# Sample's output projection as a job inside group 2, token sums added head by head, most final scalings on ACT

## The chip, the cores and the metric

One NeuronCore of one Trainium2 chip runs the program. The metric is the device time of one execution in microseconds. Engines are named as in the profile: PE multiplies matrices (PEld loads its weights), DVE, ACT and POOL are the vector, scalar and general engines, SP and POOL issue most of the DMAs. A name with a q (SPq, POOLq) is an engine's queue of issues.

## The reference

One layer over 1024 prompt tokens and 128 sample tokens (8 streams of 16), all in f32. The input is normalised and projected to q, k, v and gate of 8 stick-breaking heads (`sb`) and 8 retention heads (`ret`). Each branch's output is normalised per head, multiplied by the gain and SiLU of the gate, and both go through one output projection, are normalised and added to x:

```
def merge(o_sb, o_r, gate_sb, gate_r, g_sb, g_r, w_out):
    y_sb = head_rms_norm(o_sb, g_sb, gate_sb.dtype) * jax.nn.silu(gate_sb)
    y_r = head_rms_norm(o_r, g_r, gate_r.dtype) * jax.nn.silu(gate_r)
    y = jnp.concatenate([y_sb, y_r], axis=-1)
    return jnp.einsum('bte,ed->btd', y, w_out)
...
        xp = xp + rms_norm(out, norm_post[l])
```

## The kernel before

Tokens are worked in two groups: group 0 has prompt tiles 0 to 3 and the sample tile, group 1 (here called group 2, the second) has prompt tiles 4 to 7. For each group the heads follow one another; a written list (`order`, lines 203 to 214) gives the steps. rq, rk, rv, rg are the retention head's projections, q, k, v, sg the stick-breaking head's, x both value projections for two heads, ret starts a retention job.

Every product is made of three f32r products: each operand is split into a high part (ACT, line 137) and a low part (DVE, line 138). Weights come in blocks of 256 KB, `wr`, with four buffers, and their parts `wh` and `wl` with four each. A block of w_in feeds twelve matmuls of 512 columns.

Whatever is not a projection is a *job* (lines 164 to 184): a generator that does a piece and says after how many product steps it wants to go on. `tick()` counts a step after each product and lets one job go on, so that the jobs' instructions come to lie between the products. `drain` ticks until a job is done, with no products between. All engines work in order.

Head h of group 2: `stick_breaking` (line 657) computes scores (z), weights (sigmoids, a scan and a product into `be`), writes `be` to DRAM and reads it back in 32x32 blocks (`s_be`, lines 568 to 584), turns them on DVE into `kp` (line 587) and multiplies with the values (line 705). `finish` (line 631) normalises the head's output, takes it through DRAM in the same way, multiplies with the gate (line 649) and stores it to `s_y` (line 652).

Sample's output projection is four steps of the list, o4 to o7 (`do_o`, line 1166): 16 blocks of w_out each, and per block three matmuls into `acco` (line 1179). o4 follows head 4, o5 head 5, o6 and o7 stand in head 7 behind ret7. Their results go to `s_raw`; Sample's normalisation and addition of x (`finish_sample`, line 1392) comes in the final product.

The prompt's output projection is a block product in Winograd's form: tokens (group 0, group 2), heads (sb, ret) and output columns are halved, and seven products of sums replace eight. Sums of weights are made by the job `column_sums` (line 1216) and stored in `s_t`. Sums of token blocks, S1, S2, s3 and s4, are made by DMA alone in `row_sums` (line 1236): copies and adding copies of 1 MB, DRAM to DRAM, on POOL's queue. row_sums(0), heads 0 to 3, is a job from q6 of group 2; row_sums(1) is one in the final product. There are four units (two halves of the heads, two of the columns) of seven products of 48 matmuls, in the order "1265734", in the last unit "1265374"; each operand is loaded (`fill`, line 1246) and split (`cut`, line 1253) one or two products ahead. Product "1" of the first unit still belongs to the stretch of head 7.

At the end every output tile t (8) and column block c (4) is scaled by its row's factor and x is added, in one DVE instruction (line 1362), and stored: tiles 0 to 3 from `finish_first` (line 1384) behind product "3", tiles 4 to 7 one after the other during the last product "4".

## Time and profile before

| | |
|---|---|
| median of 3 runs | 2402.28 us (2400.89 to 2404.65) |
| the profiled execution | 2402.57 us, span 2400.9 us |
| PE busy | 2294.6 us, 13920 matmuls |
| DVE, ACT, POOL busy | 1423.1, 914.1, 544.0 us |
| DMA moved | 477.25 MB, 199 GB/s on average |

Times in the trace count from the span's start. A group line gives line, engine, operation, out<-in, count, busy time, mean ns, and the idle time of the engine just before with what ended it. A timeline line gives start, duration, engine, line, operation and, in brackets, the idle time before it and what released it. A line of waits gives the total, how often, and the longest.

### The profile page before, as it was taken

The page shows a single profiled execution, that of the slowest core. Times are in us where ns is not written, and L with a number is a line of the kernel's source. Part 1 is how long each engine was busy: PE and PEld are TensorE (multiplying, and loading weights), DVE is VectorE, ACT ScalarE, POOL GpSimd, SP SyncE. Part 2 cuts the span into 40 slices and gives each one's busy share as a digit, 9 for nine tenths or more (in the row PEclk, how much of TensorE's full clock was granted, in tenths as well). Part 3 has the DMA queues.
Part 4 walks back from the last instruction along what each step waited for, and adds up shares of the span by engine and source line. Part 5 has one row for each costly group of instructions (what it writes and reads, how often), then busy time and mean ns, then how long its engine had stood idle before and what let it go on. Part 6 is the DMA issues. An engine that isn't in the chain of part 4 may idle for free.

```text
span 2400.9 us, 38629 instructions
## 1 busy us (share of the span) xinstructions
PE 2294.6 (96%) x13920; PEld 2021.6 (84%) x13920; DVE 1423.1 (59%) x2772; ACT 914.1 (38%) x1889; POOL 544.0 (23%) x809
## 2 busy tenths in 40 slices
PE   7999999999999999999999999999999998969995
PEld 7999999999999999998888877887878876758884
DVE  8245565556455555558477767656565566535567
ACT  6333332324233332325343333434343345425342
POOL 2123231414142232414121121212122121110001
PEclk9999999999999999999999999999999999989998
DMA  7659687887779697889788988566578757775456
GB/s 244 162 140 235 159 191 169 188 194 175 182 161 231 149 202 165 192 208 238 206 238 264 271 262 251 145 155 175 157 201 229 190 169 234 246 215 184 135 203 236
DMA packets 698160, 477.25 MB, mean 199 GB/s; under 512 B 234640, under 2 KB 633232, under 8 KB 692272
## 3 DMA queue, kind: packets, MB, share of 16 engines
q1 hardware_dynamic: 623200, 316.27, 50.6%
q0 software_dynamic: 39568, 138.06, 21.2%
q10 hardware_dynamic: 35200, 20.45, 2.9%
q8 instruction: 109, 1.79, 0.3%
q14 instruction: 83, 0.68, 0.1%
HBM read 377.14 MB, written 114.29 MB: 205 GB/s over the span
## 4 chain that ended last, share of the span: by engine, by line
PE 77%; issue 7%; DMA 7%; DVE 5%; ACT 1%; POOL 1%; SPq 0%; DVEq 0%; ACTq 0%; POOLq 0%
PE acc L314 46%; PE accn L373 11%; PE a L1270 8%; PE accx L401 3%; PE pa L705 2%; PE z L672 2%; DMA wr<-w_out 1%; PE pd L841 1%; PE zc L776 1%; DMA s_s<-s_y 1%; DVE o L1362 1%; DVE kp L615 1%; DMA be<-s_bd 1%; DVE kp L587 1%; DMA out<-rawc 1%
## 5 line engine op out<-in xcount | busy, mean ns | idle before, releaser
L314 PE MATMUL acc<-mh,wh 128*128 128x256 f32 (+2 forms) x2304 | 662.0, 340 | 4.6 <-DVE rv L1156 4.1
L314 PE MATMUL acc<-mh,wl 128*128 128x256 f32 (+2 forms) x2304 | 663.1, 340 | 0.0
L314 PE MATMUL acc<-ml,wh 128*128 128x256 f32 (+2 forms) x2304 | 660.9, 339 | 0.9 <-DVE p0u L150 0.9
L138 DVE TENSOR_TENSOR wl<-wr,wh 128x512 fp32r<-128x512 f32 x432 | 296.2, 690 | 430.8 <-ACT wh L137 426.3
L137 ACT ACTIVATE wh<-wr 128x512 fp32r<-128x512 f32 x432 | 271.5, 632 | 631.5 <-PE acc L314 368.0
L314 PEld LDWEIGHTS acc<-mh,wh 128*128 128x128 f32 x2304 | 422.1, 188 | 40.3 <-issue 6.6
L314 PEld LDWEIGHTS acc<-mh,wl 128*128 128x128 f32 x2304 | 421.6, 188 | 36.9 <-issue 8.2
L314 PEld LDWEIGHTS acc<-ml,wh 128*128 128x128 f32 x2304 | 421.7, 188 | 36.3 <-issue 6.6
L757 POOL DMA_DIRECT2D kc<-cache_sb_k x256 | 166.5, 655 | 283.2 <-DVE kcT L788 131.2
L373 PE MATMUL accn<-whn,mh 128*128 128x256 f32 x768 | 223.9, 292 | 0.0
L373 PE MATMUL accn<-wln,mh 128*128 128x256 f32 x768 | 217.1, 283 | 0.0
L373 PE MATMUL accn<-whn,ml 128*128 128x256 f32 x768 | 217.0, 283 | 0.0
L373 PEld LDWEIGHTS accn<-whn,mh 128*128 128x128 f32 x768 | 146.7, 191 | 9.8 <-issue 7.9
L373 PEld LDWEIGHTS accn<-wln,mh 128*128 128x128 f32 x768 | 146.7, 191 | 0.3
L373 PEld LDWEIGHTS accn<-whn,ml 128*128 128x128 f32 x768 | 146.5, 191 | 0.0
L1270 PE MATMUL a<-wh,mh 128*128 128x512 f32 x320 | 126.2, 394 | 10.9 <-ACT wh L137 8.2
L615 DVE TENSOR_TENSOR_SCAN kp<-kp 128x640 f32<-128x640 f32 (+6 forms) x72 | 108.1, 1502 | 41.0 <-POOL kp L604 38.4
L1270 PE MATMUL a<-wl,mh 128*128 128x512 f32 x320 | 126.1, 394 | 2.3 <-DVE wl L138 2.3
L1270 PE MATMUL a<-wh,ml 128*128 128x512 f32 x320 | 125.7, 393 | 0.0
L587 DVE STREAM_TRANSPOSE kp<-be 128x640 f32<-128x640 f32 (+6 forms) x72 | 95.3, 1323 | 7.8 <-DMA be<-s_bd 5.6
L705 PEld LDWEIGHTS pa<-vn,kp 128*128 128x128 f32 x576 | 78.9, 196 | 21.8 <-DVE kp L587 16.6
L138 DVE TENSOR_TENSOR wln<-wrn,whn 128x512 fp32r<-128x512 f32 x80 | 54.9, 688 | 68.2 <-ACT whn L137 65.2
(267 smaller groups left out, 3564.5 us busy)
## 6 DMA issues: line engine op xcount, KB each, us to landing
wr<-w_in SPq DMA_DIRECT2D x384, 256.0 KB, 4.6
vc<-cache_sb_v SPq DMA_DIRECT2D x64, 512.0 KB, 7.3
wr<-w_out SPq DMA_DIRECT2D x112, 256.0 KB, 3.6
wrn<-w_in SPq DMA_DIRECT2D x80, 256.0 KB, 3.8
kc<-cache_sb_k SPq DMA_DIRECT2D x256, 64.0 KB, 4.3
kc<-cache_sb_k POOLq DMA_DIRECT2D x256, 64.0 KB, 4.6
tr<-w_out SPq DMA_DIRECT2D x32, 512.0 KB, 7.4
s_t<-ts POOLq DMA_DIRECT2D x16, 1024.0 KB, 5.2
```

The costliest lines, as they stand in the source:

```text
L137: nc.scalar.activation(hi, src, AF.Copy)
L138: nc.vector.tensor_tensor(lo, src, hi.bitcast(F32), ALU.subtract)
L314: last = nc.tensor.matmul(a[:, :m], lhs[:, j, :], rhs[w][:, j, o : o + m], start=(w == 0 and j == 0 and n == 0), stop=(w == KT // WQ - 1 a ...
L373: product[0] = nc.tensor.matmul(a, lhs[q][:, jj, ts], rhs[:, j, :], start=(w == 0 and j == 0 and n == 0 and t % 2 == 0), stop=(w == KT // ...
L401: product[0] = nc.tensor.matmul(banks[t], lhs[q][:, j, ts], rhs, start=(k == 0 and n == 0), stop=(k == KT - 1 and n == 2))
L587: place(nc.vector.transpose(dst.rearrange("p (k b j) -> p k j b", j=4, b=32), raw))
L615: nc.vector.tensor_tensor_scan(rev, rev, rev, 1.0, ALU.mult, ALU.bypass)
L672: mm = nc.tensor.matmul(z[:, :c], q2[a][:, i * P : (i + 1) * P], k2[b][:, :c], start=(m == 0), stop=(m == 2))
L705: nc.tensor.matmul(po[:, :P], at[:, j, :], rest["vn"][:, j, :], start=(j == 0), stop=(j == t))
L757: (nc.gpsimd if i < 2 else nc.sync).dma_start(kc[32 * i : 32 * i + 32, :].rearrange("p (k d) -> p k d", d=32), cache_k[0, 2 * c + j, s * 5 ...
L776: mm = nc.tensor.matmul(z[r, :], qp[:, j, r], ready[2 * j + c // 2][:, c % 2, :], start=(j == 0), stop=(j == 1),)
L1270: product[0] = nc.tensor.matmul(banks[p], a[:, k, ts], b, start=(name in "125" and k == 0 and n == 0), stop=(k == H // 2 - 1 and n == 2), ...
```

## The change

Four things are done.

1. The steps o4 to o7 leave the list. The job `sample_out`, started before rg2 of group 2, loads Sample's rows as before and then does one block (load, split, three matmuls into `sao`, a bank of another pool) every `D_SO` = 25 steps.
2. The sums of token blocks are kept for all heads in one tensor each. When the last head of group 0 is done, `row_sums` copies group 0's share. Each head of group 2 then adds its own output from SBUF in `finish`: for sb to S1, s3, S2, s4, for ret to S1, S2, s4, the first one of S1 as a plain store. The store of group 2's sb output falls away.
3. `column_sums` takes 128 steps a block in place of 72 (with steps of 4 between its parts turned to 8).
4. 24 of the 32 final scalings become an ACT instruction that scales, and a store that adds (`accum_op`) to the output, to which x was copied before by `give_x` in the third unit. Eight (columns 2 and 3 of tiles 4 to 7) stay as they were. Tiles 0 to 3 are scaled by a job, one block every 4 steps. Sample's last step moves from the second unit to the third.

```diff
 D_FIN = 4
+D_SO = 25
+D_CS = 56
...
-                "rq3 rk3 ret3 rg3 q3 k3 sg3 rq4 rk4 ret4 rg4 q4 k4 x4 sg4 o4 rq5 rk5 ret5 q5 k5 rg5 sg5 o5 "
-                "rq6 rk6 ret6 q6 k6 x6 sg6 rq7 q7 k7 rg6 rk7 ret7 o6 o7 rg7 sg7"
+                "rq3 rk3 ret3 rg3 q3 k3 sg3 rq4 rk4 ret4 rg4 q4 k4 x4 sg4 rq5 rk5 ret5 q5 k5 rg5 sg5 "
+                "rq6 rk6 ret6 q6 k6 x6 sg6 rq7 q7 k7 rg6 rk7 ret7 rg7 sg7"
...
-            def finish(self, b, h, gates, gate, dst):
+            def finish(self, b, h, gates, gate, dst, sums=0):
...
                     )
-                nc.gpsimd.dma_start(dst, gT[:, :n])
+                if dst is not None:
+                    nc.gpsimd.dma_start(dst, gT[:, :n])
+                if sums:
+                    while not run["rows"].done:
+                        yield 3
+                    for name in ("S1", "S2", "s4") if b else ("S1", "s3", "S2", "s4"):
+                        fresh = name == "S1" and h not in begun
+                        begun.add(h)
+                        nc.gpsimd.dma_start(
+                            s_sum[name][:, h, :], gT[:, :n], **({} if fresh else dict(accum_op=ALU.add))
+                        )
...
-            ret["end"] = Job(out.finish(1, h, ret, "rg", s_y[gi][:, H + h, :]), 2)
+            ret["end"] = Job(out.finish(1, h, ret, "rg", s_y[gi][:, H + h, :], gi), 2)
...
-            rest["end"] = Job(out.finish(0, h, rest, "sg", s_y[gi][:, h, : 4 * P]), 2)
+            rest["end"] = Job(out.finish(0, h, rest, "sg", None if gi else s_y[0][:, h, : 4 * P], gi), 2)
...
+                    run["rows"] = Job(row_sums(self.last), 2)
...
-            def do_o(self):
-                c = self.h - 4
-                if c == 0:
-                    drain(run["ys"])
-                bank = accp.tile([P, 512], F32, name="acco", tag=f"acc{c % 2}")
...
-                    split(wh, wl, wr)
-                    q, j = divmod(k, WQ)
-                    for n, (a, b) in enumerate(((hi, wh), (hi, wl), (lo, wh))):
-                        product[0] = nc.tensor.matmul(
-                            bank, a[q][:, j, NB_TOK:], b, start=(k == 0 and n == 0), stop=(k == KT - 1 and n == 2)
-                        )
-                        tick()
-                raw = run["tq"].tile([P, 512], F32, name="raw", tag="raw")
-                nc.scalar.activation(raw, bank, AF.Square, accum_out=ssq_s[:, c : c + 1])
-                nc.vector.tensor_copy(raw, bank)
-                nc.gpsimd.dma_start(s_raw[:, c, :], raw)
...
-        def sample_rows(mov):
+        def sample_out(mov):
...
+            hi, lo = mov
+            for c in range(4):
+                bank = psd.tile([P, 512], F32, name="sao", tag="pd")
+                for k in range(KT):
+                    wr = panel_load(k, c * 512, 512)()
+                    wh = wp.tile([P, 512], F32R, name="who", tag="wh")
+                    wl = wp.tile([P, 512], F32R, name="wlo", tag="wl")
+                    split(wh, wl, wr)
+                    q, j = divmod(k, WQ)
+                    for n, (a, b) in enumerate(((hi, wh), (hi, wl), (lo, wh))):
+                        nc.tensor.matmul(
+                            bank, a[q][:, j, NB_TOK:], b, start=(k == 0 and n == 0), stop=(k == KT - 1 and n == 2)
+                        )
+                    yield D_SO
+                raw = run["tq"].tile([P, 512], F32, name="raw", tag="raw")
+                nc.scalar.activation(raw, bank, AF.Square, accum_out=ssq_s[:, c : c + 1])
+                nc.vector.tensor_copy(raw, bank)
+                nc.gpsimd.dma_start(s_raw[:, c, :], raw)
+                yield D_SO
 
...
-                    yield D_LATE
+                    yield D_CS
                     place(nc.vector.tensor_tensor(t[:, 0], r[:, 0, 0], r[:, 0, 1], ALU.subtract))
                     nc.vector.scalar_tensor_tensor(t[:, 1], t[:, 0], -1.0, r[:, 1, 1], ALU.mult, ALU.subtract)
-                    yield D_FIN
+                    yield D_CS // 7
                     place(nc.vector.tensor_tensor(t[:, 2], r[:, 1, 1], r[:, 0, 1], ALU.subtract))
                     nc.vector.scalar_tensor_tensor(t[:, 3], t[:, 1], -1.0, r[:, 1, 0], ALU.mult, ALU.subtract)
-                    yield D_FIN
+                    yield D_CS // 7
                     place(nc.gpsimd.dma_start(s_t[u][:, k], t))
-                    yield D_LATE
-        def row_sums(q):
-            h0, h1 = slice(q * H // 2, (q + 1) * H // 2), slice(H + q * H // 2, H + (q + 1) * H // 2)
-            a11, a12, a21, a22 = (s_y[g][:, hs, :NB_TOK] for g in range(2) for hs in (h0, h1))
-            s = s_sum[q]
-            for name, first, more in (("S1", a21, a22), ("s3", a11, a21), ("S2", s["S1"], a11), ("s4", s["S2"], a12)):
-                place(nc.gpsimd.dma_start(s[name], first))
-                yield D_TI[1]
-                place(nc.gpsimd.dma_start(s[name], more, accum_op=ALU.add))
+                    yield D_CS
+
+        def row_sums(last):
+            while not all("end" in x and x["end"].done for x in (last.rest, last.ret)):
+                yield 3
+            for name in ("s3", "S2", "s4"):
+                for q in range(2):
+                    hs = slice(q * H // 2, (q + 1) * H // 2)
+                    place(nc.gpsimd.dma_start(s_sum[name][:, hs, :], s_y[0][:, hs, :NB_TOK]))
+                    yield D_TI[1]
+            for q in range(2):
+                hs, hr = (slice(d * H + q * H // 2, d * H + (q + 1) * H // 2) for d in range(2))
+                place(nc.gpsimd.dma_start(s_sum["s4"][:, hs, :], s_y[0][:, hr, :NB_TOK], accum_op=ALU.add))
                 yield D_TI[1]
 
...
-                if (gi, step, h) == (1, "rq", 3):
+                if (gi, step, h) == (1, "rg", 2):
                     drain(ends["d"])
-                    run["ys"] = Job(sample_rows(mov), 2)
-                if (gi, step, h) == (1, "q", 6):
-                    run["rows"] = Job(row_sums(0), 2)
+                    run["ys"] = Job(sample_out(mov), 2)
                 if (gi, step, h) == (1, "rg", 7):
-                    drain(run["rows"])
+                    drain(run["ys"])
                     drain(run["sums"])
                 getattr(heads[h], "do_" + step)()
 
...
-        def scale(t, c, rs, q):
+        def scale(t, c, rs):
             o = outs[t][c]
             cs = slice(c * 512, (c + 1) * 512)
-            nc.vector.scalar_tensor_tensor(o, o, rs, xrs[t][:, cs], ALU.mult, ALU.add)
-            q.dma_start(y_rows(t)[:, cs], o)
+            if added(t, c):
+                nc.scalar.activation(o, o, AF.Copy, scale=rs)
+                acc = nc.gpsimd.dma_start(y_rows(t)[:, cs], o, accum_op=ALU.add)
+                tc.add_manual_dep(acc.ins, xs_given[t].ins.name, SYNC, reason="adds to what was copied")
+            else:
+                nc.vector.scalar_tensor_tensor(o, o, rs, xrs[t][:, c - 2, :], ALU.mult, ALU.add)
+                nc.sync.dma_start(y_rows(t)[:, cs], o)
+
+        def added(t, c):
+            return t < 4 or c < 2
+
+        xs_given = {}
+        SYNC = mybir.DependencyInfo(mybir.DependencyClass.Sync, mybir.DependencyReason.DATA)
+
+        def give_x():
+            for t in range(PT):
+                part = x_rows(t) if added(t, 3) else x_rows(t)[:, :1024]
+                to = y_rows(t) if added(t, 3) else y_rows(t)[:, :1024]
+                xs_given[t] = nc.gpsimd.dma_start(to, part)
+                place(xs_given[t])
+                yield 24
 
...
+            yield 2
             for t in range(4):
                 for c in range(4):
-                    scale(t, c, rs[:, t : t + 1], nc.gpsimd)
+                    scale(t, c, rs[:, t : t + 1])
+                    yield 4
 
         def finish_sample():
...
+            if n == 2:
+                given_x = Job(give_x(), 2)
...
-                        for cc in range(4):
-                            scale(t, cc, u_, nc.sync)
+                        for cc in (2, 0, 3, 1):
+                            scale(t, cc, u_)
...
                 if final and name == "3":
-                    finish_first()
+                    firsts = Job(finish_first(), 2)
                 if final and name == "7":
                     rest[0] = rest_of(x2)
-                if n == 1:
+                if n == 2:
                     next(sample, None)
                     next(sample, None)
...
-                if final and name in ROWS_AT:
-                    t, q = ROWS_AT[name]
-                    for i, s in enumerate("hl"):
-                        xr = mp.tile([P, D], F32, name="xr", tag=f"m{s}{q}")
-                        nc.gpsimd.dma_start(xr, x_rows(t + i))
-                        xrs[t + i] = xr
+                if final and name == "1":
+                    for i, tag in enumerate(("mh0", "ml0")):
+                        xr = mp.tile([P, 2, 2, 512], F32, name="xr", tag=tag)
+                        for j in range(2):
+                            t = 4 + 2 * i + j
+                            nc.gpsimd.dma_start(xr[:, j], x_rows(t)[:, 1024:].rearrange("p (c e) -> p c e", c=2))
+                            xrs[t] = xr[:, j]
+                if final and name == "6":
+                    drain(given_x)
                 step += 1
```

The order of instructions follows. On PE in group 2, behind sg4, before: a whole step of blocks (acco is o's bank, acc a projection's; who and wlo are the parts of a block of w_out).

```order
L314 MATMUL acc_18200<-mh_13249,wl 128x512
L1179 MATMUL acco<-who,mh_12881 128x512
L705 MATMUL pa<-vn,kp 128x128 x4
L1179 MATMUL acco<-wlo,mh_12881 128x512
L1179 MATMUL acco<-who,ml_12882 128x512
L896 MATMUL pS<-rv,rkn 128x128
L1179 MATMUL acco<-who,mh_12881 128x512
```

And now: in the middle of a value projection (accx), one block of three (sao), then the projection again.

```order
L401 MATMUL accx_15880<-whx,mh_13245 128x512
L401 MATMUL accx_15880<-wlx,mh_13245 128x512
L1216 MATMUL sao<-who,mh_12877 128x512
L1216 MATMUL sao<-wlo,mh_12877 128x512
L1216 MATMUL sao<-who,ml_12878 128x512
L401 MATMUL accx_15880<-whx,ml_13246 128x512
L401 MATMUL accx_15877<-whx,mh_13245 128x512
```

The 192 matmuls of o are in threes between 25 others. On PE behind product "1" of the first unit, the end of head 7, before (pa is the bank of the values' products, a a bank of the final product):

```order
L1270 MATMUL a_21591<-wl_21601,mh_21524 128x512
L705 MATMUL pa<-vn,kp 128x128 x4
L1270 MATMUL a_21591<-wh_21600,ml_21525 128x512
L1270 MATMUL a_21592<-wh_21600,mh_21524 128x512
L1270 MATMUL a_21592<-wl_21601,mh_21524 128x512
L705 MATMUL pa<-vn,kp 128x128 x4
L1270 MATMUL a_21592<-wh_21600,ml_21525 128x512
L1270 MATMUL a_21593<-wh_21600,mh_21524 128x512
```

And now:

```order
L1283 MATMUL a_21565<-wh_21683,mh_21434 128x512
L1283 MATMUL a_21565<-wl_21684,mh_21434 128x512
L1283 MATMUL a_21565<-wh_21683,ml_21435 128x512
L717 MATMUL pa<-vn,kp 128x128 x15
L1283 MATMUL a_21837<-wh_21847,mh_21489 128x512
L1283 MATMUL a_21837<-wl_21848,mh_21489 128x512
L1283 MATMUL a_21837<-wh_21847,ml_21490 128x512
```

Two lots of value products, 7 and 8, now stand together behind all 48 matmuls of product "1", ahead of product "2". On ACT in the last unit, behind the factor of tiles 0 to 3 (outr; wh are the parts of the last two weight blocks), now:

```order
L1372 ACTIVATE o_3_21807<-o_3_21807,outr 128x512
L1372 ACTIVATE o_0_21808<-o_0_21808,outr 128x512
L1365 ACTIVATE sq_24077,ssq_21832<-o_3_21819 128x512
L1372 ACTIVATE o_1_21809<-o_1_21809,outr 128x512
L1365 ACTIVATE sq_24086,ssq_21832<-o_3_21823 128x512
L1372 ACTIVATE o_2_21810<-o_2_21810,outr 128x512
L1365 ACTIVATE sq_24095,ssq_21832<-o_3_21827 128x512
L1372 ACTIVATE o_3_21811<-o_3_21811,outr 128x512
L1365 ACTIVATE sq_24104,ssq_21832<-o_3_21831 128x512
L139 ACTIVATE wh_24126<-wrt 128x512
L139 ACTIVATE wh_24132<-wrt 128x512
L1372 ACTIVATE o_0_21812<-o_0_21812,outr 128x512
```

Before, the two splits followed the factor at once and no scalings stood there.

22 lines of the change are left out of this document (6 added, 16 removed).

## The prediction, made before the result was known

> **What bounds the kernel now.** I read the page first, then who waits for whom on PE, then busy time by stretches, then the timeline of the stretches with losses.
>
> ```profile
> PE 2294.6 (96%) x13920; PEld 2021.6 (84%) x13920; DVE 1423.1 (59%) x2772; ACT 914.1 (38%) x1889; POOL 544.0 (23%) x809
> PE   7999999999999999999999999999999998969995
> ```
>
> PE is the bound nearly everywhere, so a change pays only where PE waits. The slices say where: the start, two slices near the end and the last one. The waits name the work:
>
> ```profile
> PE acco L1179 <- ACT who L137: 11.7, 8, 3.4
> PE a L1270 <- DVE wl L138: 11.4, 6, 8.9
> PE a L1270 <- ACT wh L137: 8.7, 3, 7.8
> PE acco L1179 <- DVE wlo L138: 7.2, 13, 1.8
> PE a L1270 <- DVE o L1351: 6.7, 1, 6.7
> ```
>
> Three places stand behind them: Sample's output projection (acco), one unit of the final product (wl, wh) and the last scalings (o L1351). The change touches all three. In stretches (length, then busy time and count of PE, PEld, DVE, ACT, POOL, then PEclk, DMA share, GB/s):
>
> ```profile
> 1662.00:1682.00 20.00, 16.59 (x78) 11.59 (x77) 13.85 (x27) 11.59 (x23) 1.18 (x1) 1.00 0.65 190
> 1756.00:1780.00 24.00, 18.44 (x59) 12.52 (x58) 15.72 (x26) 10.67 (x19) 5.72 (x6) 0.79 0.71 204
> 1780.00:1860.00 80.00, 80.00 (x380) 66.71 (x379) 45.57 (x74) 31.26 (x61) 20.49 (x25) 1.00 0.89 232
> 1860.00:1959.00 99.00, 98.46 (x478) 82.58 (x477) 58.03 (x106) 39.27 (x85) 18.44 (x24) 1.00 0.62 167
> 1959.00:1984.00 25.00, 19.35 (x71) 12.51 (x69) 17.23 (x25) 13.46 (x26) 5.41 (x7) 0.93 0.79 237
> 1984.00:2009.00 25.00, 16.52 (x73) 12.64 (x72) 16.04 (x26) 10.74 (x25) 3.44 (x3) 0.93 0.57 176
> 2095.00:2150.00 55.00, 35.15 (x131) 26.36 (x130) 19.06 (x28) 11.02 (x18) 9.84 (x15) 0.84 0.79 221
> ```
>
> Four of these (20, 24, 25 and 25 us) hold o4 to o7; between them PE is full. Busy time understates the loss, since a matmul record is longer at a lowered clock, so I count matmuls at their start-to-start time instead:
>
> ```profile
> L1179 PE MATMUL acco<-who,mh x64: 389/397/632, 1662.2 to 2007.0; 128*128 128x512 f32 x64
> 1639.70 0.39 PE L401 MATMUL accx<-whx,mh 128*128 128x512 f32 x1
> 1639.92 0.39 PE L401 MATMUL accx<-wlx,mh 128*128 128x512 f32 x1
> 1988.31 1.90 ACT L137 ACTIVATE who<-wr 128x512 fp32r<-128x512 f32 x3 [4.26 <-DMA wr<-w_out]
> ```
>
> A full-rate matmul of 512 columns takes 0.227 us. One 256 KB block of w_out feeds three of them here, 0.68 us of PE, but needs one split on ACT and one on DVE (0.63 and 0.69 us, below) and a load with four buffers; ACT waits for the loads. A block of w_in feeds twelve, 2.72 us. That is why o stalls and the other projections don't.
>
> ```profile
> L138 DVE TENSOR_TENSOR wl<-wr,wh 128x512 fp32r<-128x512 f32 x432 | 296.2, 690 | 430.8 <-ACT wh L137 426.3
> L137 ACT ACTIVATE wh<-wr 128x512 fp32r<-128x512 f32 x432 | 271.5, 632 | 631.5 <-PE acc L314 368.0
> ```
>
> **Term A, the projection spread.** The same 192 matmuls, 64 loads and 64 splits stay; they move to every 25th product step of group 2, from rg2 to the end of head 6. The four stretches are 94 us long and hold 281 matmuls: 192 of o at 0.227 are 43.6 us, the other 89, mostly of 128 columns, about 12.5 at a mean of 0.14. The loss is 94 - 56 = 38 us. Some 3 us of it belong to other waits, leaving 35 to be had. Spread, a block of 0.68 us comes between 25 steps of 5.7 us: DVE's extra 0.69 us in 6.4 raises its load (58.03 of 99 us in the row of 1860) by a tenth, ACT's likewise, and the loads come to (25 / 12 + 1) x 256 KB in 6.4 us, 124 GB/s. The cover is there, but a sample block takes one of four weight buffers and holds only three matmuls, so the lead of the splits falls from 48 to some 39 matmuls. I charge 3 us (bounds 0 and 10). A = +32 (25 to 35).
>
> **Term B, the token sums.** Now one unit of the final product loses 55 - 131 x 0.227 = 25 us:
>
> ```profile
> 2107.64 1.22 POOL L1243 DMA_DIRECT2D s_S<-s_y  x1 [7.69 <-DMA s_S<-s_S]
> 2119.11 0.69 DVE L1403 TENSOR_TENSOR rawc<-rawc,gpost 128x512 f32<-128x512 f32 x1 [9.83 <-DMA rawc<-s_raw]
> 2121.24 0.79 PE L1270 MATMUL a<-wl,a22h 128*128 128x512 f32 x1 [8.85 <-DVE wl L138]
> 2141.14 1.06 ACT L1256 ACTIVATE mh<-ml 128x1024 fp32r<-128x1024 f32 x1 [13.59 <-DMA ml<-s_y]
> 2145.65 0.80 PE L1270 MATMUL a<-wh,mh 128*128 128x512 f32 x1 [7.75 <-ACT wh L137]
> ```
>
> row_sums(1) is a chain of 1 MB copies and additions on POOL's queue, each waiting for the one before; the loads of rawc and of the next operand stand behind it, DVE and ACT wait for these in order, and the splits behind them come late. In the change this chain is gone from the final product; the sums are added head by head in group 2, where POOL's waits cost little (in 1780 to 1860, with the first such chain, PE is busy 80.00 of 80). Sample's last step moves to the third unit, where eight copies of x into the output stand before its rawc loads. They depend on nothing and come 24 steps, 5.4 us, apart, so I charge 4 us (0 to 12) and 1 us that stays. B = +20 (12 to 24).
>
> **Term C, the tail.**
>
> ```profile
> 2061.67 2.07 ACT L1349 ACTIVATE o<-a 128x512 f32<-128x512 f32 x4 [2.84 <-DVE sg L649]
> 2359.20 10.69 DVE L1362 SCALAR_TENSOR_TENSOR o<-o,outr,xr 128x512 f32<-128x512 f32 x16
> 2370.64 0.77 PE L1270 MATMUL a<-wh,a22h 128*128 128x512 f32 x1 [6.68 <-DVE o L1351]
> 2394.27 2.74 DVE L1362 SCALAR_TENSOR_TENSOR o<-o,lastu,xr 128x512 f32<-128x512 f32 x4
> ```
>
> DVE sets the end: 16 scalings in a row hold the banks that PE waits 6.68 us for, and four scalings a tile close it. Moving 24 of 32 takes 24 x 0.67 = 16 us from DVE and puts 24 x 0.52 = 12.4 us on ACT. I walk the new order from the moment the factor is ready (2359.2): ACT works off twelve scalings, four squares and two splits until +11, PE ends the last product at +15.5, and the addition, square and factor of the last tile, behind the scalings of the three before it, take both engines to +25, the landing to +28, against 41.7 now: 14 us gained, if the stores keep up. ACT's splits of the last two weight blocks now stand behind twelve scalings, which costs PE about 1 us of that. The stores are the doubt. A plain 256 KB store can be priced, an accumulating one from SBUF appears nowhere, one from DRAM does. DMA in 2361 to 2374 (16 plain stores on POOL's queue), in 2108.6 to 2118.6 (one 1 MB addition and one 256 KB load) and in 2384 to 2400 (16 plain stores on SP's), each as packets, MB, share of 16 engines:
>
> ```profile
> q0 software_dynamic: 1280, 4.20, 88.5%
> q0 software_dynamic: 607, 1.31, 72.6%
> q1 hardware_dynamic: 2304, 4.20, 78.2%
> ```
>
> A plain store takes all engines for 0.885 x 13 / 16 = 0.72 us. The addition takes (7.26 - 0.72) / 4 = 1.6 us per 256 KB. At 0.72 the 24 stores never queue up. At 1.6 they need 38.4 us from about 2361 on, the 8 plain ones 6.2 more, and the end comes at 2407, 6 us after now. Its destination is read and added as in the second case, only its source is nearer, so I take 1.3: 24 x 1.3 + 6.2 = 37.4 us, and an end near 2400. C = +1 (-6 to +14).
>
> The Trainium skill, "Collectives: The Full Stack" (the section on the bandwidth ceiling), says that an addition in the DMA path is slower because it reads two sources, not because of the adding. By that the source's place is no help, the price is 1.6, and the sum is 7 us less, as in the first rival; the trace agrees so far as its addition takes twice a plain store.
>
> **Term D, head 7 loses its cover.** o6 and o7 stood behind ret7, and their 96 product steps gave head 7 time. They go, so the last rows of stick-breaking are turned at the end of the first product:
>
> ```profile
> 1992.35 0.56 PE L672 MATMUL z<-kh,ql 128*128 128x512 f32 x1
> 2009.03 0.50 SPq L574 DMA_DIRECT2D s_be<-be  x1
> 2036.08 1.99 DVE L587 STREAM_TRANSPOSE kp<-be 128x1024 f32<-128x1024 f32 x1
> L1257 DVE TENSOR_TENSOR ml<-ml,mh 128x1024 fp32r<-128x1024 f32 x8 | 9.7, 1219 | 3.6 <-ACT mh L1256 3.6
> 2061.89 0.56 POOL L652 DMA_DIRECT2D s_y<-sg  x1 [10.54 <-DVE sg L649]
> 2073.65 2.01 ACT L1256 ACTIVATE mh<-ml 128x1024 fp32r<-128x1024 f32 x2 [4.88 <-DMA ml<-s_s]
> ```
>
> From the last scores to the end of that transpose are 46 us now, 17 of them only because the write was placed late. In the new order some 78 full matmuls and a few small ones, 21 us, lie between these scores and the 15 value products that PE issues in one go. DVE has the eight cuts of the operands (9.7 us), six splits, the retention of head 7 and two transposes to do in between, about 24 us, with scan, product and transpose some 30. PE waits 9 us (0 to 25). Next is the head's end: from the transpose to its store are 24 us, now under the first product, then beginning behind it. On POOL's queue the load of s3 stands behind it, and took 9.5 us to its cut; the cut stands among the splits of "5", due 27 us after the first product. I charge 7 us (0 to 14). D = -16 (-5 to -35).
>
> **Sum.** 32 + 20 + 1 - 16 = +37: a span of 2400.9 - 37 = 2364. This execution took 2402.57 us with its span, 1.7 us around it, and stands within 0.3 us of the median of 2402.28. I predict **2365 us**.
>
> **The rivals.**
> 1. The accumulating stores queue up at 1.6 us each and set the end. For it: the only row of an addition; the eight final ones on POOL stand in the same queue behind sixteen. Against: their source is SBUF. C = -6, so 2372.
> 2. Head 7 stands bare: nothing of the 46 us is saved but the 21 under matmuls, and the head's end costs its 14. For it: in 2009 to 2035 the operands' loads, ACT and DVE are as dense as anywhere. Against: 17 of the 46 us were placement. D = -39, so 2389.
> 3. Slower: the additions in group 2 do there, head by head, what they did in 2095 to 2150. Place: POOL's queue, where reads of turned rows stand behind seven stores a head. Two additions of 1 MB cost 25 us there, 12.5 a MB; 14 MB are added in group 2. It decides from 37 / 14 = 2.7 us a MB; at 6 it is about 2450, at 12.5 about 2540. Against: in 1780 to 1860 such a chain cost PE nothing.
> 4. Spreading saves nothing, because each block waits for its own load wherever it stands. For it: ACT waits for DMA at o. Against: w_in's blocks pass through the same buffers without a wait. A = -3, so 2400.
> 5. Better: the new end of group 2 costs 5, the stores keep up: 32 + 22 + 12 - 5 = 61, so 2341.
>
> **How the numbers follow.** Forecast 0.50, first rival 0.15, second 0.10, third 0.06, fourth 0.05, better 0.14. The range of 2335 to 2390 holds the forecast, the first rival, the better case and about half of the second. A difference under 0.2% (4.8 us) can't be told from none. Slower: the third, 0.06. Same: the fourth, 0.05. Faster: 0.89.
>
> **What would show it.** A: no PE wait on the new product line over 1 us, and no stretch of group 2 with under 95% of PE before head 7. B: the unit after 2060 at full rate, small DVE waits for rawc in the third unit. C: the last stores' time to landing; over 10 us says that they queue up. D: a PE wait of about 9 us for the transpose before 15 value products, and one before "5". The forecast is wrong if PE loses over 20 us in heads 0 to 6, or if the end of group 2 costs more than 35.

## The result

The change made the kernel slower, by half a percent. It takes 2415.63 us (median of 4 runs, 2412.43 to 2416.39) against 2401.79 for the kernel before; the ratio is 1.0053 with a 95% interval of 1.0036 to 1.007. The profiled execution has a span of 2414.1 us, 13.2 more than before.

The page and PE's waits of the changed kernel, each wait with its total, how often, and the longest:

```profile
PE 2286.4 (95%) x13920; PEld 2024.8 (84%) x13920; DVE 1406.1 (58%) x2748; ACT 932.1 (39%) x1915; POOL 594.9 (25%) x861
PE   7999999999999999999997999999999998799695
...
PE a L1283 <- ACT mh L1269: 19.4, 1, 19.4
PE pa L893 <- DVE sc L877: 18.4, 3, 13.7
PE pa L717 <- DVE kp L587: 14.1, 7, 3.5
...
PE a L1283 <- ACT o L1358: 11.2, 1, 11.2
...
PE sao L1216 <- DVE wlo L140: 3.3, 2, 1.8
```

The waits of before on acco, wl and wh are gone but for 1.8 us on wl and wh, and of the new product line (sao) 3.3 us are left. The 14.1 us for turned rows (kp) are no new loss, they were 12.8 before, but they lie in other places. New losses stand in four places: the slice of 7 in the middle (about 1290 us), the end of group 2, the third unit of the final product, and the last slices. To see what each is worth, I cut both executions at the same matmuls and compare lengths. Stretches between the same cuts (length, then busy time and count of PE, PEld, DVE, ACT, POOL, then PEclk, DMA share, GB/s), of the kernel before:

```profile
1264.20:1300.50 36.30, 36.30 (x191) 30.95 (x190) 24.79 (x58) 14.09 (x34) 3.44 (x4) 1.00 0.80 239
1368.00:2035.50 667.50, 633.04 (x2968) 519.24 (x2967) 413.46 (x734) 275.64 (x571) 129.25 (x155) 0.98 0.70 197
2035.50:2095.80 60.30, 57.24 (x257) 46.53 (x256) 37.98 (x70) 29.57 (x47) 8.71 (x13) 1.00 0.77 259
2095.80:2264.40 168.60, 148.75 (x625) 120.22 (x624) 82.00 (x116) 63.05 (x99) 15.43 (x23) 0.94 0.60 188
2264.40:2297.00 32.60, 32.60 (x145) 27.02 (x144) 21.04 (x34) 14.59 (x31) 0.75 (x1) 1.00 0.38 121
2352.90:2400.90 48.00, 24.25 (x97) 19.25 (x95) 41.08 (x85) 11.92 (x34) 9.71 (x18) 0.80 0.65 229
```

and of the changed one:

```profile
1268.80:1327.00 58.20, 41.15 (x191) 34.23 (x190) 29.53 (x67) 17.31 (x37) 8.24 (x8) 0.82 0.74 184
1392.00:2027.00 635.00, 615.98 (x2925) 513.11 (x2924) 412.77 (x732) 273.85 (x558) 148.58 (x183) 0.99 0.79 217
2027.70:2112.30 84.60, 66.58 (x297) 54.31 (x296) 45.65 (x89) 32.49 (x61) 11.28 (x14) 0.90 0.64 179
2112.30:2253.70 141.40, 141.40 (x625) 117.11 (x624) 73.96 (x106) 60.77 (x96) 8.26 (x13) 1.00 0.53 182
2253.70:2308.40 54.70, 35.28 (x145) 28.21 (x145) 27.28 (x41) 16.57 (x32) 9.63 (x17) 0.81 0.59 196
2362.90:2414.10 51.20, 22.26 (x97) 17.71 (x95) 25.45 (x61) 26.18 (x58) 20.99 (x24) 0.74 0.87 174
```

The same 191 matmuls at the start of group 2 take 58.2 us in place of 36.3; group 2 up to its last projection 32 us less; the end of group 2 24 more; the units behind it, with the same 625 matmuls, 27 less and without a gap; the third unit's second half 22 more; the tail 3 more. The second and third rows don't hold quite the same work: 40 small matmuls (value products of head 7 and some of its retention), which stood ahead of the cut before, stand behind it now (297 matmuls in place of 257). They start 0.11 us apart in the trace, so by an estimate 4.4 us of the 32 less and of the 24 more are moved work and no gain or loss. This holds for every kernel below but e6.

The table gives these stretches for every kernel below, each against the execution of before, with cuts at the start of a fixed projection matmul (numbers 4736 and 5376 of the lines that write acc), of the first, sixth, 19th, 22nd and 27th full product of the final product, and the end. The column "units 1 to 3" reaches from the sixth to the 18th product, so the first four products of the third unit are in it. All entries are differences of start times in the traces. The change was run four times, e9 to e11 four times and e12 five times; e1 to e8 and e13 were run once.

| stretch, us against before | start | start of group 2 | rest of group 2 | its end | units 1 to 3 | third unit, end | last unit | tail | span |
|---|---|---|---|---|---|---|---|---|---|
| the change | +5.7 | +18.7 | -32.2 | +24.3 | -27.1 | +22.0 | -1.4 | +3.2 | 2414.1 |
| e1 paced copies | +3.9 | +45.1 | -35.6 | +27.0 | -27.1 | +22.5 | -1.5 | +3.0 | 2438.2 |
| e2 Sample in unit 2 | +0.3 | +18.8 | -29.6 | +26.9 | -22.7 | +7.7 | -1.5 | +3.0 | 2403.8 |
| e3 plain stores | -1.0 | +14.9 | -30.2 | +27.4 | -27.1 | +22.2 | -1.5 | -7.2 | 2398.4 |
| e4 old tail | +0.4 | +16.5 | -29.4 | +26.6 | -27.1 | 0.0 | +0.2 | 0.0 | 2388.1 |
| e5 direct stores | +5.8 | -5.9 | -22.1 | +25.1 | -27.1 | +22.3 | -1.5 | +3.3 | 2400.7 |
| e6 half spread | -0.8 | +17.4 | -13.4 | +10.1 | -27.1 | +22.2 | -1.5 | +3.4 | 2411.2 |
| e7 spread alone | +1.9 | +1.2 | -24.9 | +17.4 | -5.3 | 0.0 | -0.6 | +0.4 | 2391.0 |
| e8 direct, old tail | +6.0 | -2.1 | -18.9 | +25.7 | -27.1 | 0.0 | -0.4 | -0.1 | 2383.8 |
| e9 twelve adding | +6.3 | -7.8 | -18.1 | +27.9 | -27.1 | 0.0 | +0.1 | -0.3 | 2381.8 |
| e10 the same, quick | +9.7 | -6.1 | -19.7 | +10.2 | -27.1 | 0.0 | -0.3 | -0.1 | 2367.5 |
| e11 e8, quick | +5.9 | -6.7 | -18.4 | +8.5 | -27.1 | 0.0 | -0.5 | +0.1 | 2362.8 |
| e12 adds early, quick | +5.8 | -7.7 | -25.5 | +10.5 | -27.1 | 0.0 | +0.5 | -2.7 | 2354.6 |
| e13 idle copies | +13.4 | +21.0 | -25.3 | +26.7 | -27.1 | +23.4 | -0.8 | +3.4 | 2435.5 |

The first column differs by some 6 us between kernels whose code for that stretch is the same (the change, e2, e3 and e4): that much of the change's 13.2 us can be an execution's own scatter. But the seven kernels in which group 0's heads store into the sums themselves (e5, e8 to e13) all have +5.8 or more there. In them PE waits 4.7 to 10.1 us in all for turned rows of sample heads (pd) ahead of that cut, against 0.9 in before and 0.5 to 4.8 in the others. So these stores probably cost a few us in group 0; no run isolates it. Which half of a loss falls into "start" or "rest" of group 2 varies too, so I read those two columns together where it matters.

**Start of group 2.** The timeline of POOL (start, duration, engine, line, operation, idle time before and its releaser) and the one row of DVE that PE waits for:

```profile
1250.53 1.51 POOL L662 DMA_DIRECT2D s_S<-rg  x2
1251.68 1.14 POOL L1252 DMA_DIRECT2D s_s<-s_y  x1
...
1253.43 1.15 POOL L1252 DMA_DIRECT2D s_s<-s_y  x1
1278.04 1.17 POOL L574 DMA_DIRECT2D s_rk<-rk  x1 [23.45 <-DVE rk L434]
1279.20 1.36 POOL L1256 DMA_DIRECT2D s_s<-s_y  x1
1279.99 1.13 POOL L1243 DMA_DIRECT2D s_t<-ts  x1
1280.55 1.88 POOL L1256 DMA_DIRECT2D s_s<-s_y  x1
...
1301.50 1.08 DVE L587 STREAM_TRANSPOSE rkn<-ro 128x512 f32<-128x512 f32 x1 [14.14 <-DMA ro<-s_rk]
```

The six copies of group 0's share, 1 MB each (L1252), leave from 1206 to 1254, four of them ahead of these rows. The two additions (L1256) leave just behind the write of head 1's keys (s_rk), while these make their trip through DRAM. The DMA issues of 1250 to 1305, with the median from issue to landing, and the same read in the kernel before (1230 to 1300):

```profile
s_s<-s_y POOLq DMA_DIRECT2D x4, 1024.0 KB, 12.5
ro<-s_rk SPq DMA_DIRECT2D x1, 256.0 KB, 18.6
```

```profile
ro<-s_rk SPq DMA_DIRECT2D x1, 256.0 KB, 2.7
```

The read of 256 KB lands after 18.6 us in place of 2.7; DVE waits 14.14 us for it, in order, with sc behind it, and PE 13.7. The read stands on SP's queue, not on POOL's.

**End of group 2.** ACT's first eviction of the final product waits for the end of head 7:

```profile
2074.16 2.06 ACT L1358 ACTIVATE o<-a 128x512 f32<-128x512 f32 x4 [9.85 <-DVE sg L651]
```

PE waits 11.2 us for this instruction, and twice, 2.2 and 2.8 us, for turned rows in this stretch. Before, the eviction came at 2061.67 after a wait of 2.84, 26 us after the start of the first product; now it comes 46 us after it.

**Third unit.**

```profile
2211.22 1.03 POOL L1389 DMA_DIRECT2D out<-x_prompt  x2
2212.52 0.57 POOL L1430 DMA_DIRECT2D rawc<-s_raw  x1 [0.26 <-issue]
...
2213.61 0.51 POOL L1389 DMA_DIRECT2D out<-x_prompt  x1
2269.82 0.56 POOL L1435 DMA_DIRECT2D out<-rawc  x1 [55.70 <-DVE rawc L1434]
...
2274.56 0.77 POOL L1264 DMA_DIRECT2D ml<-s_s  x1
...
2267.57 0.68 DVE L1433 TENSOR_TENSOR rawc<-rawc,gpost 128x512 f32<-128x512 f32 x1
...
2283.05 2.00 ACT L1269 ACTIVATE mh<-ml 128x1024 fp32r<-128x1024 f32 x2 [15.19 <-DMA ml<-s_s]
```

POOL waits 55.7 us with the store of Sample's first columns, because DVE's order has the scaling (L1433) only behind the evictions of product "7", at 2267. The load of s4 (ml) stands behind that store and leaves at 2274.56; its buffer was free when product "2" ended, at 2232. ACT waits 15.19 us for it, and PE 19.4 for ACT.

**Tail.** ACT ends its last scaling at 2394.9; then only stores run. DMA of the changed kernel in 2380 to 2390 (packets, MB, share of 16 engines; then stores with their median time to landing):

```profile
q0 software_dynamic: 1126, 2.05, 112.9%
...
out<-o POOLq DMA_DIRECT2D x8, 256.0 KB, 11.2
```

2.05 MB are 7.8 stores in 11.3 us of all engines: 1.44 us each. They queue up until 2411.

### The profile page after: what moved, and what is told of

Read it like the earlier page. It is cut to its first block, busy times and chain, and to the rows that moved or that the text cites. A ratio compares the mean times of both kernels' runs of the same rounds, so it can differ in the third digit from the quotient of the medians.

```text
span 2414.1 us, 38660 instructions
## 1 busy us (share of the span) xinstructions
PE 2286.4 (95%) x13920; PEld 2024.8 (84%) x13920; DVE 1406.1 (58%) x2748; ACT 932.1 (39%) x1915; POOL 594.9 (25%) x861
## 3 DMA queue, kind: packets, MB, share of 16 engines
q0 software_dynamic: 47824, 144.35, 23.4%
## 4 chain that ended last, share of the span: by engine, by line
PE 76%; issue 7%; DMA 7%; DVE 4%; ACT 2%; POOL 2%; SPq 1%; POOLq 0%; DVEq 0%; ACTq 0%
PE acc L314 43%; PE accn L373 10%; PE a L1283 10%; PE accx L401 2%; PE pa L717 2%; PE z L684 2%; DMA be<-s_bd 1%; PE pd L853 1%; PE sao L1216 1%; PE zc L788 1%; DMA wr<-w_in 1%; DMA ro<-s_rk 1%; DMA s_o<-so 1%; DVE kp L587 1%; DVE kp L615 1%
## 5 line engine op out<-in xcount | busy, mean ns | idle before, releaser
L314 PEld LDWEIGHTS acc<-ml,wh 128*128 128x128 f32 x2304 | 423.2, 189 | 36.3 <-issue 6.6
L1283 PE MATMUL a<-wh,mh 128*128 128x512 f32 x320 | 127.5, 398 | 32.2 <-ACT mh L1269 19.4
L587 DVE STREAM_TRANSPOSE kp<-be 128x640 f32<-128x640 f32 (+6 forms) x72 | 95.1, 1321 | 27.9 <-DMA be<-s_be 16.1
L1283 PEld LDWEIGHTS a<-wh,mh 128*128 128x128 f32 x320 | 61.5, 192 | 46.4 <-ACT mh L1269 19.8
L574 POOL DMA_DIRECT2D s_o<-so x16 | 19.3, 1208 | 317.8 <-DVE kp L593 229.6
```

The lines of the kernel that those rows point to most:

```text
L314: last = nc.tensor.matmul(a[:, :m], lhs[:, j, :], rhs[w][:, j, o : o + m], start=(w == 0 and j == 0 and n == 0), stop=(w == KT // WQ - 1 a ...
L587: place(nc.vector.transpose(dst.rearrange("p (k b j) -> p k j b", j=4, b=32), raw))
L1283: product[0] = nc.tensor.matmul(banks[p], a[:, k, ts], b, start=(name in "125" and k == 0 and n == 0), stop=(k == H // 2 - 1 and n == 2), ...
```

## The experiments

**e1, copies further apart.**

```diff
-                    yield D_TI[1]
+                    yield D_RS      # 100
```

> The change, with the eight 1 MB copies and additions of group 0's share 100 product steps (23 us) apart in place of 34 (8 us). Theory (the batch fills the DMA engines from 1206 to 1301 us, so that the turned rows of head 1's keys, ro, land 18.6 us after their issue): the loss of 22 us between 1269 and 1327 us falls under 5 us and the time is about 2395 us. Rival (the additions that each head issues on POOL's queue hold back the turned rows, whatever the copies do): the loss stays or moves to a later head, 2410 us or more.

2439.94 us; the loss stays, which was to be the rival's sign. The start of group 2 loses 45 us. The heads' ends wait for all eight transfers, and a step that needs such an end drains the rest: three copies leave together, and both additions. So the copies were not spaced after all. From POOL's timeline:

```profile
1273.25 1.14 POOL L1252 DMA_DIRECT2D s_S<-s_y  x1
1274.02 1.87 POOL L1252 DMA_DIRECT2D s_s<-s_y  x2
...
1308.97 2.68 POOL L1256 DMA_DIRECT2D s_s<-s_y  x2
```

So the run doesn't separate the load of the copies from the heads' wait for them; e5 and e13 do.

**e2, Sample's last step in the second unit.**

```diff
-                if n == 2:
+                if n == 1:
                     next(sample, None)
```

> The change, with Sample's last step back in the second unit of the final product. Theory (in the third unit the load of s4 stands on POOL's queue behind the store of Sample's first columns, and that store waits for DVE, which does its work behind the evictions of a product; in the second unit every operand's load stands ahead of such a store): the wait of 19.4 us of PE for mh is gone, no wait over 5 us takes its place in the second unit, 2396 us. Rival (Sample's step costs some 20 us wherever it stands, as it did in the second unit before the change): 2413 us or more.

2405.94 us, 10 less than the change against the 20 expected. The wait for mh falls from 19.4 to 4.1 us (once). The theory of the order holds, and the step is free in the second unit, whose seven products take 10.9 us each. What stays is 12 us in the third unit, 4.4 of them in the column ahead of it, and only the copies of x are left there. Eight copies leave in two lots of four, and at the first lot ACT waits 10.57 us for a block of weights. POOL and ACT:

```profile
2211.17 1.97 POOL L1389 DMA_DIRECT2D out<-x_prompt  x4
2236.83 0.80 POOL L1264 DMA_DIRECT2D ml<-s_s  x1 [23.69 <-PE a L1283]
2237.62 2.06 POOL L1389 DMA_DIRECT2D out<-x_prompt  x4
...
2230.82 0.63 ACT L139 ACTIVATE wh<-wr 128x512 fp32r<-128x512 f32 x1 [10.57 <-DMA wr<-w_out]
```

**e3, plain stores.** Twenty-four blocks of the output lack x.

```diff
-                acc = nc.gpsimd.dma_start(y_rows(t)[:, cs], o, accum_op=ALU.add)
+                acc = nc.gpsimd.dma_start(y_rows(t)[:, cs], o)
```

> The change, with the 24 stores of ACT's scalings plain in place of adding (x is left out of those outputs; the copies of x stay). Theory (an adding store takes the 16 engines 1.42 us, 24 of them and 8 plain ones 40 us, and this queue sets the end): at 0.72 us a store nothing queues up, the end comes 25 to 28 us after the factor of the first tiles, as the walk of the engines gives, about 2402 us. Rival (the scalings on ACT or the fixed time of a store to landing set the end): 2411 us or more.

2400.08 us; the tail is 10.4 us shorter. DMA of 2352 to 2398.4:

```profile
q0 software_dynamic: 1920, 6.29, 36.3%
...
out<-o POOLq DMA_DIRECT2D x24, 256.0 KB, 4.4
```

24 plain stores take 0.363 x 46.4 / 24 = 0.70 us each, half of 1.44, and land in 4.4 us in place of 10.5. The adding stores set the end of the changed kernel.

**e4, the tail of before**, and so no copies of x; Sample's step stays in the third unit.

```diff
-                nc.scalar.activation(o, o, AF.Copy, scale=rs)
-                acc = nc.gpsimd.dma_start(y_rows(t)[:, cs], o, accum_op=ALU.add)
+            nc.vector.scalar_tensor_tensor(o, o, rs, xrs[t][:, cs], ALU.mult, ALU.add)
+            q.dma_start(y_rows(t)[:, cs], o)
...
-                given_x = Job(give_x(), 2)
```

> The change, with the tail of before: 32 scalings with their addition on DVE, plain stores, x loaded and not copied to the output; Sample's last step stays in the third unit. Tail: 3 us less than in the change, if the changed tail cost that. Third unit: if the copies of x on POOL's queue ahead of Sample's loads cause the wait of 19.4 us, it falls under 5 us and the time is about 2392 us; if the place of Sample's stores ahead of the load of s4 causes it, the wait stays over 12 us and the time is about 2411 us.

2389.81 us. The third unit loses nothing, and the tail is what it was. In the order of this kernel Sample's store is still ahead of the load of s4, but DVE's scaling now comes 14 us behind its load in place of 55:

```profile
2209.20 0.55 POOL L1409 DMA_DIRECT2D rawc<-s_raw  x1 [0.32 <-ACT wh L139]
...
2224.97 0.55 POOL L1414 DMA_DIRECT2D out<-rawc  x1 [14.69 <-DVE rawc L1413]
...
2230.09 0.76 POOL L1264 DMA_DIRECT2D ml<-s_s  x1 [0.38 <-PE a L1283]
```

So the loss comes with the copies of x. In the change it is the order that comes out with them; without Sample's step beside them (e2) the copies still cost 12 us in this unit. Why the order puts the scaling so late is in no trace. This run changes the tail as well; e9 has adding stores and Sample's step in the third unit, with half the copies in the second, and loses nothing there either.

**e5, group 0's heads store into the sums themselves.**

```diff
+                names = (("S1", "S2", "s4") if b else ("S1", "s3", "S2", "s4")) if sums else (("s4",) if b else ("s3", "S2", "s4"))
+                for name in names if self.nt >= 4 else ():
+                    fresh = (name, h) not in begun
...
-                    run["rows"] = Job(row_sums(self.last), 2)
```

> The change without the copies of group 0's share: each head of group 0 stores its own output from SBUF into the sums (plain stores to s4 for ret, to s3 and S2 for sb, an addition to s4 for sb) in its finish, and no head waits for the copies. The run with spaced copies did not free the stretch, since heads that wait for the copies drain the rest of them in one go. Theory (the batch of copies fills the DMA engines and, by the wait for it, holds up the ends of heads 0 and 1): the loss of 22 us between 1269 and 1327 us is gone, and the time is 2390 to 2396 us. Rival (the additions per head in group 2 do it): the loss stays, 2410 us or more.

2402.47 us, above the 2390 to 2396 expected. The start of group 2 is 24.6 us shorter than in the change (-5.9 against +18.7), though the additions of group 2's heads are all there, so they are not what stalled. Ten of these are missing again in the rest of group 2 (-22.1 against -32.2): I read that as work that the stalled start had let the other engines finish early, which no run isolates. Both columns together, the change loses 14.5 us against this run.

**e6, two of Sample's steps back in head 7.**

```diff
-                "rq6 rk6 ret6 q6 k6 x6 sg6 rq7 q7 k7 rg6 rk7 ret7 rg7 sg7"
+                "rq6 rk6 ret6 q6 k6 x6 sg6 rq7 q7 k7 rg6 rk7 ret7 o6 o7 rg7 sg7"
...
-            for c in range(4):
+            for c in range(2):
```

> The change, with two of Sample's four column steps back in head 7 behind ret7 as before, and two spread. Theory (the end of group 2 lost 24 us because head 7 lost the cover of 96 product steps): from the last projection product to the sixth product of the final product the loss falls from 24 to about 7 us, and the two steps in one piece lose some 19 us themselves, so the time stays within 6 us of the change. Rival (the additions at the end of group 2 and their queue cost it, not the cover): the end stays at 20 us or more and the two steps cost their 19 us on top, 2430 us or more.

2412.92 us. The end of group 2 loses 10.1 us in place of 24.3, and group 2 gains 13.4 in place of 32.2: that is 14 us for the cover and 19 for the two steps in one piece. Here the 40 small matmuls stay ahead of the cut, so 4.4 us of both are moved work: some 10 and 14. The theory holds.

**e7, the spread alone, on the kernel before.**

```diff
-                "rq3 rk3 ret3 rg3 q3 k3 sg3 rq4 rk4 ret4 rg4 q4 k4 x4 sg4 o4 rq5 rk5 ret5 q5 k5 rg5 sg5 o5 "
+                "rq3 rk3 ret3 rg3 q3 k3 sg3 rq4 rk4 ret4 rg4 q4 k4 x4 sg4 rq5 rk5 ret5 q5 k5 rg5 sg5 "
...
-                    run["ys"] = Job(sample_rows(mov), 2)
+                    run["ys"] = Job(sample_out(mov), 2)
```

> The kernel before with the first part of the change alone: Sample's output projection as a job of one block every 25 steps, sums and tail as before. Prediction: a gain of 32 us for the four stretches and a loss of 16 at the end of group 2. Measured in the change: gain 34, loss 24, so theory: 2392 us, with the loss at the end of group 2 at 20 to 25 us. Rival (that loss came from the additions of heads 6 and 7): it is under 12 us here, 2380 us or less.

2392.7 us: 8 to 10 less than before. The end of group 2 loses 17.4 us with no addition of a head anywhere near, between the theory's 20 to 25 and the rival's 12: most of the 24.3 is the cover. The other 7 are in PE's wait for the first eviction, 4.5 us here in place of 11.2; what makes it longer in the change no run isolates. The gain in group 2 is 25 here. The transfers of row_sums(0), which cost PE nothing in 1780 to 1860 before, now do:

```profile
PE pa L706 <- DVE kp L588: 8.9, 1, 8.9
```

That wait (at 1814 us) begins 8 us after an addition and a copy of 1 MB left together; DVE stands for a split of ACT, and the weight blocks issued beside the two took 10 and 13 us to land.

**e8, direct stores and the old tail.**

> The change with the direct stores of group 0's heads (as in the first kernel of this set) and the tail of before, no copies of x. If the three losses are independent (22 at the start of group 2, 22 in the third unit, 3 at the tail): 2414 - 47 = 2367 us of span, 2369 us. If the freed time at the start is given back later in group 2: 2385 us or more.

2385.57 us, where the second expectation had it: part of the time that is freed at the start is given back later. The third unit and the tail give back all of their 25 us, the start its 21, but the rest of group 2 falls from -32 to -19.

**e9, twelve adding stores**, with the direct stores of e5.

```diff
-            return t < 4 or c < 2
+            return c < (2 if t >= 4 else 1)
...
-            if n == 2:
+            if n == 1:
                 given_x = Job(give_x(), 2)
```

> Direct stores of group 0's heads, Sample's last step in the third unit, x copied in the second unit, and 12 adding stores in place of 24 (column 0 of tiles 0 to 3, columns 0 and 1 of tiles 4 to 7), 20 scalings on DVE. Theory (an adding store costs 1.42 us of all engines, a plain one 0.72, a scaling on DVE 0.69, and the largest of the sums sets the end): the stores need 12 x 1.42 + 20 x 0.72 = 31 us, DVE about 32, so the end comes some 34 us after the factor of tiles 0 to 3 in place of 45 (24 adding) and 42 (none); against the run with direct stores and the old tail that is 7 us less, about 2378 us. Rival (the last tile's chain sets the end anyway): 2384 us or more. If the copies of x in the second unit hold its loads back as they did in the third, 2395 us.

2383.62 us (ratio to before 0.9924, 0.9907 to 0.994): within half a microsecond of the rival's 2384. The tail is as long as the old one. The copies of x, half the bytes and in the second unit, cost nothing.

**e10 and e11, shorter distances at the end of head 7**, on e9 and on e8.

```diff
+                if (gi, h, i) == (1, H - 1, 3):
+                    a, b, c, d = 28, 30, 22, 8
...
-                yield D_TO[phase[0]]
+                quick = phase[0] and b == 0 and h == H - 1
+                yield 24 if quick else D_TO[phase[0]]
```

> The kernel with 12 adding stores, with shorter distances for the last row of head 7 (write 28 steps behind its scores in place of 32, read 30 behind the write in place of 50, turn 22 behind it in place of 38, values 8 behind it in place of 12) and for its end (24 and 20 in place of 40 and 34). Theory (part of the 25 us at the end of group 2 is placement): 8 us less than without, about 2370 us. Rival (DMA landings and engines in order set that chain): within 3 us of the kernel without.

> Direct stores and the old tail, with the same shorter distances for head 7. From the last scores of head 7 to the first eviction of the first product are some 54 us in the run without. Theory: 8 us less, 2377 us. Rival: within 3 us of 2385.6.

2369.05 us (0.9861, 0.9846 to 0.9876) and 2367.14 us (0.9854, 0.984 to 0.9869), 15 and 18 us less than without where 8 was expected: the end of group 2 loses 10.2 and 8.5 us in place of 27.9 and 25.7. The eviction that PE waits for comes 34 us after the start of the first product in place of 47. In e8 and in e11:

```profile
2067.62 2.06 ACT L1342 ACTIVATE o<-a 128x512 f32<-128x512 f32 x4 [9.53 <-DVE sg L651]
```

```profile
2050.36 2.06 ACT L1345 ACTIVATE o<-a 128x512 f32<-128x512 f32 x4 [2.33 <-DVE sg L652]
```

Most of the loss was distance that had been written for a place with cover.

**e12, the adding stores early**, on e10.

```diff
-            return c < (2 if t >= 4 else 1)
+            return c < (1 if t >= 4 else 3)
```

> Direct stores, shorter distances for head 7, and 16 adding stores of which 12 come early: columns 0 to 2 of tiles 0 to 3 and column 0 of tiles 4 to 7; 16 scalings on DVE. In the run with 12 adding stores, eight of them among the last 16 stores, the DMA engines stood idle from 2358 to 2361 us and then worked until the end. Theory (the bytes and additions of the last 16 stores set the end, so the additions belong ahead of them): early 12 x 1.42 + 4 x 0.72 = 20 us are over before the last product, late 4 x 1.42 + 12 x 0.75 = 15 us in place of 17 to 18, and DVE does 2.8 us less between; 4 us less than the old tail with the same shorter distances, 2361 to 2363 us. Rival (the time from the last product's end to the last landing is fixed by the chain of the last tile): within 2 us of 2367 us.

2364.54 us (median of 5; ratio 0.984, 0.9821 to 0.986). The profiled tail is 2.7 us shorter than the old one, but that execution is the fastest of the five. The intervals of e12 and e11 overlap, so in time the two can't be told apart, and neither the theory nor the rival is shown. With e11 it is the fastest kernel of this study, 1.6% under before and 2.1% under the change.

**e13, idle copies beside the direct stores**, into tensors that nobody reads, no wait for them.

```diff
+                    run["rows"] = Job(row_sums(self.last), 2)
...
-                    place(nc.gpsimd.dma_start(s_sum[name][:, hs, :], s_y[0][:, hs, :NB_TOK]))
+                    place(nc.gpsimd.dma_start(s_dum[name][:, hs, :], s_y[0][:, hs, :NB_TOK]))
```

> The kernel with direct stores of group 0's heads, and beside them the eight copies and additions of 1 MB as the change issues them, at the same distances, into tensors that nobody reads; no head waits for them. Theory (the batch of transfers itself fills the DMA engines): the loss of 22 us between 1269 and 1327 us is back, 2415 to 2425 us. Rival (what stalled were heads 0 and 1, whose ends waited for the copies): the loss stays under 6 us, 2402 to 2407 us.

2437.26 us, 12 above the most that was expected. The start of group 2 loses 26.9 us against e5, which has the same sums without these transfers; the read ro takes 17.3 us again, against 4.4 in e5:

```profile
ro<-s_rk SPq DMA_DIRECT2D x1, 256.0 KB, 17.3
```

```profile
ro<-s_rk SPq DMA_DIRECT2D x1, 256.0 KB, 4.4
```

The load alone does it: here no head waits for these transfers. It works through more than this one read, for PE waits 7.6 us behind it and 10.4, in three waits, for other turned rows. Another 7.6 us against e5 appear before that place, in group 0, little more than the scatter there.

## Why the prediction was wrong

I predicted 2365 us and a gain of 37; it became a loss of 13. The difference of 50 us lies in a term that was not there (the copies of group 0's share, 19 us), in one that was mis-sized five times over (Sample's step with the copies of x in the third unit, 22 against 4), and in two that were mis-sized within their bounds.

**Term A, the spread: right in kind, and its number in part luck.** Predicted +32, measured +32.2, of which some 4.4 are moved work. Alone (e7) the column shows 25, and behind a start that does not stall (e5, e8) 22 and 19, with the same 4.4 in each. So the full 32 is not the worth of the spread by itself. The waits on the new line were 1.8 and 1.5 us.

**Term B, the sums: the removed part right, the added part missed.** The final product's second unit runs at full rate: +27.1 against the 25 that I read from before. Two things fell:

- The prediction costed the additions per head in group 2, at nothing, and they did cost nothing visible (e5). It did not cost the copies of group 0's share, six of 1 MB and two additions that `row_sums` now issues in 76 us (1206 to 1282) at the start of group 2. The row that I leaned on (PE at 80.00 of 80 beside such a chain) showed one place where no turned rows were due. Here they were: without these transfers and the wait for them the start is 25 us shorter (e5), and with the transfers alone it is 27 longer again (e13). My third rival came nearest (transfers on POOL's queue against the reads of turned rows), but it hung the loss on the heads' additions, and on a place behind them in the queue. The read that came late stood on SP's queue, and took 18.6 us to land.
- Sample's step with the copies of x was charged 4 us (0 to 12), "they depend on nothing". What they changed was the order: DVE's scaling moved behind product "7", Sample's store waited for it, and the load of s4 behind that store. It cost 22.0 us; without the copies 0.0 (e4). As transfers they were priced too low as well: they did not come 5.4 us apart but up to four at a time, and cost 12 us with no step of Sample's beside them (e2). The order of the changed kernel showed both rows, and I read only POOL's.

**Term C, the tail: mechanism right, price too low.** I took 1.3 us for an adding store, because its source is nearer; it is 1.44, against 0.70 plain. The Trainium skill, "Collectives: The Full Stack" (the section on the bandwidth ceiling), has a reduction at half the rate of a gather, which copies, because its addition reads two sources; the trace agrees, the ratio here is 2.06. SBUF as a source helps little, 1.44 us against my estimate of 1.6 from DRAM. C was -3.2, about midway between my +1 and the first rival's -6. Both ends in the prediction, 2400 and 2407, hold some 1.4 us more than the terms it names (2361 + 38.4 + 6.2 is 2405.6). My walk of the engines was right: 25 us from the factor (2369.2) to the end of the last scaling, measured 25.7 (2394.9). With plain stores the tail is 7.2 us shorter than before (e3) and not 14: from the last scaling (2389.7) to the end are 8.7 us there, where I had allowed 3 for a landing.

**Term D, the lost cover: right in kind, too small.** -16 predicted, -24.3 measured, within -5 to -35; without the moved work it is some -20. Before the value products PE waited 2.2 and 2.8 us for turned rows, where I had 9. The step that failed is the head's end. I let it bind through the load of s3 (7 us); it bound through the first eviction, which waits for head 7's last product with the gate (11.2 us), a row that I had quoted for another purpose (o at 2061.67, 2.84 behind sg). e10 and e11 take back 17 to 18 us by the distances alone, so most of this loss was placement. The prediction had named 17 us of placement too, but in the write, which these runs bring forward by 4 steps only; that the two numbers agree is chance.

**The signs.** A's failed in both parts: the new line's two waits are over 1 us (1.8 and 1.5), and the start of group 2 has PE busy for 41.15 of 58.20 us, though the rest of it for 97%. D's came in another form: no wait of 9 us and none before "5", but 2.2 and 2.8 us and the 11.2 behind "1". B's first sign came (full rate after 2112), the second failed (19.4 us for mh, not small waits of DVE). C's sign said that over 10 us to landing means a queue: 10.5 us.

**The sum.** With the measured terms, 32.2 + 27.1 - 22.0 - 18.7 - 24.3 - 3.2 - 5.7 + 1.4 = -13.2. Against the prediction, B is short by 34 (+20 predicted; 27.1 - 22.0 - 18.7 = -13.6 measured), D by 8 and C by 4; 4 us are the first and the last-unit columns together. The third unit and the copies of group 0's share decide it.

## What to carry to other kernels

Work that is moved out of a bad place brings its preparation along: list every transfer that the new arrangement issues, with its place, before calling the additions cheap. A bulk transfer that nothing waits for is not free where other work makes short trips through DRAM, and a quiet row elsewhere does not show that it is. When cover is moved away, the distances that were written for it must be shortened with it; here that was worth 17 us, more than half of what the move gained.

## What the runs showed of the hardware

- A store from SBUF that adds to DRAM takes the 16 DMA engines 1.44 us per 256 KB, a plain one 0.70 (e3); I had expected 1.3, and had estimated 1.6 for an addition from DRAM.
- With two additions of 1 MB just issued, the read of 256 KB in small blocks took 17.3 and 18.6 us to land (e13, the change) in place of 2.7 and 4.4 (before, e5), and DVE and PE stood behind it in order.
